# Second norm by pairs of token blocks, and three units of the up projection begun by products without sums

## The chip, the cores and the metric

The kernel runs on one core of a Trainium2 chip. Its engines are TensorE (PE, matmuls; the loading of its weights is shown as PEld), VectorE (DVE), ScalarE (ACT), GpSimd (POOL) and SyncE (SP), on whose queue all of the kernel's DMAs are issued. The metric is the device time of one execution in microseconds (us). A profile of one execution gives the start and length of each instruction.

## What is computed

One layer of a hybrid backbone on 1024 tokens of width 1024. Attention and retention with their gates make `merged`; after that, cut to what matters here:

```
x   = x + g1 * (merged @ w_out)                   # w_out 1024 x 1024
hx2 = rmsnorm(x) * norm2_g * (1 + sc2) + sh2      # the second norm
u   = hx2 @ w_up                                  # 1024 x (2 x 2816)
u   = centred conv of width 3 over tokens + bias
a, val = split(u);  y = (silu(a) * val) @ w_down  # 2816 x 1024
out = rmsnorm(x + g2 * y) * final_g
```

All of it is float32. A product of two float32 matrices is made of three matmuls on halves: each operand is split into a high part (rounded to the type fp32r) and a low part (what is left), and high x high, high x low and low x high are summed in PSUM.

## The kernel before, in words

**The output projection** (`out_proj`, L1638) takes eight blocks `tb` of 128 tokens. Each has two halves `dh` of 512 columns, each a chain of 8 x 3 matmuls of 128x512 into a bank `om` (two buffers in the pool `po`). DVE multiplies the bank by the gate into `xn` (L1650; two buffers of 128x1024), adds the residual into `x1` (L1651), SP stores `x1`, ACT squares it with a sum (L1654), DVE and POOL make the reciprocal root (L1655, L1656), and DVE writes the normed row into `xn` (L1657).

**The second norm** (`norm_out`, L1660) of block `tb-1` is written behind the whole of block `tb`. PE transposes the eight 128x128 squares of `xn` into two banks `tp` (L1671); for each, ACT writes the high part of scale times square plus shift (L1677), DVE writes the same as float32 into `v` (L1679) and from it the low part (L1680). The tokens are two halves: for half 0 (`h2[0]`, tile `h2a`) `v` is stored to `d_h`; for half 1 (`h2[1]`, tiles `h2h`, `h2l`) the `v` of the block four earlier is loaded into `vo`, and four differences (L1686 to L1689) of 128x512 make one block of T1, T2, T3 and T4, which SP stores to `d_t` (L1691).

**The up projection** runs over 22 units, in the order of `seq`; a unit is one block of 128 columns of the gate half (branch 0) and of the value half (branch 1) of `u`. The operand has four quarters, B11, B21 (half 0, the two halves of the contraction) and B12, B22 (half 1); the weights of a unit have four quarters a11, a12, a21, a22. A *plain* unit multiplies both branches by both halves: 4 chains of 8 x 3 matmuls, 96 of them, each into PSUM tiles of two banks (`u_tile`, L1709). The other units need seven products of 4 x 3 matmuls instead of eight (`Seven.step`, L1401, `Up`, L1789), 84 in all: POOL makes four sums s1 to s4 of the weights (L1383 to L1386), and the products are

- step 0: a11 B11 into bank X, copied by ACT to `p1` (L1408)
- step 1: s2 T2 into Y; DVE writes `u2` = Y + p1 (L1411)
- step 2: s1 T1 into Z
- step 3: s3 T3 onto Y; `u3` = Y + p1 (L1417); Z + u3 is the output of branch 1, half 1 (L1398)
- step 4: a12 B21 onto X, which is the output of branch 0, half 0 (copied by ACT, L1819)
- step 5: a22 T4 onto Y; Y + p1 is branch 1, half 0
- step 6: s4 B22 onto Z; Z + u2 is branch 0, half 1; then the convolution of the unit (`conv`, L1754: two ACT and two times two DVE passes, a silu, a product)

Steps of neighbouring units are interleaved: the sort key of step k of unit i is 7 i + 2 k (`interleaved`, L1434). Before each product ACT and DVE split its weights into a tile `wc` (L86, L87; six buffers). T1 to T4 are loaded from `d_t` and split once for all units (`comb`, L1780; tile `T`). Their raws, the weights and the sums of weights all take tiles of one pool, `ur` and `s` in the profile, with twelve slots that are given out in the order of the program (`ur_load`, L1733). `p1`, `u2`, `u3` and `h2h`, `h2l` are tiles of a pool of 17 (`gtile`, L1563, tag g).

The first two units are plain (`PLAIN = 2`). Half 0 of the first is written ahead of the norm of the last block (`early`), its half 1 and the whole second unit behind it; T2 and T1 are loaded in the first unit, T3 and T4 in the second.

**What sets the order.** The instructions are written down in the order of the program; a planner with a model of the times gives each engine its fixed order, and puts in the waits. On one engine an instruction that waits holds up all that stand behind it. An instruction wrapped in `late` stays at its place.

Of the kernel before, what the change touches and what calls it, by code (L numbers as in the profile page):

```python
# [40 lines left out]
def tile_hybrid_layer(ctx, tc: tile.TileContext, io, dbg=None):  # L41
# [18 lines left out]
    d_h = dram.tile([NTB // 2, P, KB, P], F32, name="d_h")  # L60
    d_t = dram.tile([4, NTB // 2, P, KB // 2, P], F32, name="d_t")
# [1314 lines left out]
    class Seven:  # L1376
# [24 lines left out]
        def step(self, n):  # L1401
# [7 lines left out]
            elif n == 1:  # L1409
                self.prod(self.Y, self.s2, "T2", True, False)  # L1410
# [219 lines left out]
    h2 = [[h2p.tile([P, 2, 512], F32R, tag="h2", bufs=KB, name="h2a") for _ in range(KB)], None]  # L1630
# [7 lines left out]
    def out_proj(tb):  # L1638
# [4 lines left out]
        for dh in range(2):  # L1643
            cs = slice(dh * 512, dh * 512 + 512)
            m = po.tile([P, 512], F32, tag="o", bufs=2, name="om")
            for kb in range(KB):
                wc = wo[kb, dh]
                h_, l_ = mg[kb, half]
                mm3(m, h_[:, ts], l_[:, ts], wc[:, 0], wc[:, 1], kb == 0, kb == KB - 1)
            vec.tensor_tensor(xr[:, cs], m, gate1[:, cs], ALU.mult)  # L1650
            vec.tensor_tensor(x1[:, cs], xr[:, cs], x1[:, cs], ALU.add)  # L1651
# [6 lines left out]
        return xr  # L1658

    def norm_out(tb, xr):  # L1660
        half, ts = tb // 4, slice((tb % 4) * P, (tb % 4 + 1) * P)
        if tb == 4:
            h2[1] = [(gtile(0, F32R, "h2h"), gtile(0, F32R, "h2l")) for _ in range(KB)]
        vr = op.tile([P, KB, P], F32, tag="v", bufs=2, name="v")
        if half:
            vo = op.tile([P, KB, P], F32, tag="vo", bufs=1, name="vo")
            sync.dma_start(vo, d_h[tb - 4])
        for kg in range(2):
            tp = po.tile([P, 4, P], F32, tag="t", bufs=2, name="tp2")
            for k in range(4):  # L1670
                pe.transpose(tp[:, k], xr[:, (kg * 4 + k) * P : (kg * 4 + k + 1) * P], ident)  # L1671
            for k in range(4):
                kb = kg * 4 + k
                t = h2[half][kb]
                h_, l_ = (t[:, 0, ts], t[:, 1, ts]) if half == 0 else (t[0][:, ts], t[1][:, ts])
                a, sh = a2[:, kb : kb + 1], col[:, 24 + kb : 25 + kb]
                act.activation(h_, tp[:, k], AF.Identity, bias=sh, scale=a)  # L1677
                v = vr[:, kb]
                vec.tensor_scalar(v, tp[:, k], a, sh, ALU.mult, ALU.add)  # L1679
                vec.tensor_tensor(l_, v, h_.bitcast(F32), ALU.subtract)  # L1680
        if half == 0:
            sync.dma_start(d_h[tb], vr)
            return

        (b11, b21), (b12, b22) = [(t[:, : KB // 2], t[:, KB // 2 :]) for t in (vo, vr)]
        vec.tensor_tensor(b11, b12, b11, ALU.subtract)  # L1686
        vec.tensor_tensor(b12, b22, b12, ALU.subtract)
        vec.tensor_tensor(b22, b22, b11, ALU.subtract)
        vec.tensor_tensor(b21, b21, b22, ALU.subtract)  # L1689
        for c, t in enumerate((b11, b22, b12, b21)):  # L1690
            sync.dma_start(d_t[c, tb - 4], t)  # L1691

    xr = None
    for tb in range(NTB):
        nx = out_proj(tb)
        if tb:
            norm_out(tb - 1, xr)
        xr = nx


    def up(u, wu, half):
        h = h2[half]
        hi, lo = ([t[:, i] for t in h] if half == 0 else [t[i] for t in h] for i in range(2))
        mm_a(u[:, half * 512 : half * 512 + 512], wu, lambda k: hi[k], lambda k: lo[k])

    def up_load(j, br):
        return [wload(io["w_up"][j, br, i]) for i in range(2)]

    def u_tile(n):  # L1709
        return pu[n // 2 % 2].tile([P, T], F32, tag="u", bufs=2, name="u")  # L1710

    early = []
    for br in range(2):
        early.append((u_tile(br), up_load(0, br)))
        up(*early[br], 0)
    norm_out(NTB - 1, xr)
# [63 lines left out]
    def comb(c):  # L1780
        t = [tpl.tile([P, 4, KH, P], F32R, name=f"T{c}{i}") for i in range(2)]
        for b in range(4):
            raw = ur_load(d_t[c, b])
            split(t[0][:, b], t[1][:, b], raw.rearrange("p (k t) -> p k t", k=KH))
# [4 lines left out]
    class Up(Seven):  # L1789


        def __init__(self, n, j):
            self.n, self.j = n, j
# [7 lines left out]

        def banks(self):
            t = u_tile(2 * self.n)
            self.X, self.Y = t[:, 0:512], t[:, 512:1024]
            self.Z = u_tile(2 * self.n + 1)[:, 0:512]
            self.u = [tap.tile([P, T], F32, tag="uu", bufs=4, name="uu") for _ in range(2)]

        def moving(self, c):
            if c[0] == "T":
                h_, l_ = combs[c]  # L1810
                return [(h_[:, :, k], l_[:, :, k]) for k in range(KH)]
            k0, half = HALVES[c]
            return [(t[:, 0], t[:, 1]) if half == 0 else t for t in h2[half][k0 : k0 + KH]]

        def dst(self, b, half):
            return self.u[b][:, half * 512 : half * 512 + 512]
# [4 lines left out]
        def done(self, b, half):  # L1821
            if (b, half) == (0, 1):
                conv(self.j, *self.u)
# [11 lines left out]
    seq = [j + NH * i for j in range(NH) for i in range(2)]  # L1835
# [251 lines left out]
```

## Time and profile before

| what | us |
|---|---|
| three runs | 1766.35, 1765.24, 1760.98 |
| median | 1765.24 |
| profiled execution, first to last instruction (span; the only time kept of it) | 1759.2 |
| output projection, first matmul to last (`om`) | 1007.8 to 1100.8 |
| plain units, first matmul to last | 1101.6 to 1147.8 |
| first product by sevens | 1147.6 |

The profile lists, for each engine, groups of instructions as `line engine operation tile<-operands`, with count, busy time and mean length; waits as `who <- for whom`; and timelines, where a row is start, length, engine, line, operation, with the idle time before it and what ended it in brackets. The length of a matmul contains its way through the array, so that one starts before the other has ended; from start to start is what a matmul costs in a row of them. Times are counted from the first instruction.

### The profile page before, as it was taken

The numbers are of one execution on the slowest core, as the hardware profiler recorded it, in microseconds if no ns is written. First come the engines' busy times: TensorE is split into PE (matmuls) and PEld (weight loads), VectorE is DVE, ScalarE is ACT, GpSimd is POOL, SyncE is SP. The second block draws the span as 40 slices with busy tenths as digits, with TensorE's granted clock in tenths as the row PEclk, the third lists the DMA queues.
The fourth block names the chain that finished last, engine by engine and source line by source line (L and its number), as shares of the span: only waits on it lengthen the run. The fifth ranks groups of instructions, "written<-read, shape, count | busy, mean of one in ns | idle before, by whom it ended". The sixth has DMA issues, their size and how long they took to land.

```text
span 1759.2 us, 24801 instructions
## 1 busy us (share of the span) xinstructions
PE 1726.0 (98%) x8405; PEld 1429.3 (81%) x8405; DVE 1284.2 (73%) x2454; ACT 849.2 (48%) x1826; POOL 539.3 (31%) x455
## 2 busy tenths in 40 slices
PE   8999999999999999999999999989999999999997
PEld 4688988888888888778888888778888888788886
DVE  4778887756776766777665557868899889875755
ACT  5666666653443434443444324534444444554444
POOL 1000000003334343555413300165555655211444
PEclk9999999999999999999999999999999999999999
DMA  9143334342231212677557733733322332586754
GB/s 348 61 130 125 95 117 147 117 133 87 73 108 43 72 42 68 203 238 239 200 199 268 246 143 132 254 108 102 108 90 92 118 120 90 170 296 192 239 162 162
DMA packets 139408, 261.10 MB, mean 148 GB/s; under 512 B 15856, under 2 KB 28304, under 8 KB 139280
## 3 DMA queue, kind: packets, MB, share of 16 engines
q1 hardware_dynamic: 139280, 259.51, 44.3%
q8 instruction: 66, 1.08, 0.3%
q14 instruction: 62, 0.51, 0.1%
HBM read 187.34 MB, written 69.48 MB: 146 GB/s over the span
## 4 chain that ended last, share of the span: by engine, by line
PE 43%; issue 6%; DVE 4%; POOL 3%; DMA 1%; ACT 1%; SPq 0%; POOLq 0%; ACTq 0%; DVEq 0%
PE u L1374 30%; PE y L1374 4%; PE pr L112 2%; PE pr L111 2%; PE pr L110 2%; PE om L122 1%; PE om L121 1%; PE om L123 1%; POOL x L1902 1%; DVE wc L87 0%; DVE b L1350 0%; DVE v L1679 0%; POOL pd L1939 0%; DVE hxT L87 0%; POOL x L1947 0%
## 5 line engine op out<-in xcount | busy, mean ns | idle before, releaser
L1374 PE MATMUL u<-T,wc 128*128 128x512 f32 x960 | 227.1, 392 | 5.1 <-ACT pu L1408 5.1
L1374 PEld LDWEIGHTS u<-T,wc 128*128 128x128 f32 x960 | 180.6, 189 | 45.7 <-ACT pu L1408 7.9
L1374 PE MATMUL y<-wc,ahl 128*128 128x512 f32 x924 | 210.6, 389 | 2.7 <-DVE wc L87 1.8
L1374 PEld LDWEIGHTS y<-wc,ahl 128*128 128x128 f32 x924 | 173.3, 188 | 39.7 <-DVE wc L87 2.5
L87 DVE TENSOR_TENSOR wc<-ur,wc 128x512 fp32r<-128x512 f32 x137 | 122.7, 897 | 65.8 <-ACT wc L86 65.8
L86 ACT CAST wc<-ur 128x512 fp32r<-128x512 f32 x137 | 85.0, 621 | 129.7 <-PE y L1374 72.3
L111 PE MATMUL mm<-low,wc 128*128 128x512 f32 (+1 forms) x328 | 124.0, 378 | 0.0
L1374 PE MATMUL u<-h2a,wc 128*128 128x512 f32 x480 | 112.3, 389 | 0.7 <-DVE pu L1417 0.7
L110 PE MATMUL mm<-hx,wc 128*128 128x512 f32 x264 | 107.4, 407 | 0.2 <-ACT wc L589 0.2
L1374 PEld LDWEIGHTS u<-h2a,wc 128*128 128x128 f32 x480 | 90.0, 188 | 19.8 <-DVE pu L1417 1.2
L112 PE MATMUL mm<-hx,wc 128*128 128x512 f32 x264 | 105.2, 399 | 0.0
L86 ACT CAST wc<-s 128x512 fp32r<-128x512 f32 x80 | 49.7, 623 | 93.2 <-PE u L1374 88.3
L123 PE MATMUL mm<-wc,low 128*128 128x512 f32 (+1 forms) x240 | 91.2, 380 | 0.0
L1374 PE MATMUL u<-hxT,wc 128*128 128x512 f32 x384 | 89.6, 389 | 0.0
L1508 POOL TENSOR_TENSOR col<-col,bcol 128x32 f32<-128x32 f32 x1 | 0.3, 253 | 280.7 <-DVE aw L538 280.7
L87 DVE TENSOR_TENSOR wc<-s,wc 128x512 fp32r<-128x512 f32 x80 | 83.5, 1046 | 3.8 <-ACT wc L86 3.4
L1374 PEld LDWEIGHTS u<-hxT,wc 128*128 128x128 f32 x384 | 72.1, 188 | 14.9
L87 DVE TENSOR_TENSOR wc<-raw,wc 128x512 fp32r<-128x512 f32 x92 | 68.0, 746 | 17.7 <-ACT wc L86 17.7
L121 PE MATMUL mm<-wc,hx 128*128 128x512 f32 x192 | 75.2, 392 | 0.6 <-ACT r L1105 0.6
L122 PE MATMUL mm<-wc,hx 128*128 128x512 f32 x192 | 75.2, 392 | 0.0
L1383 POOL TENSOR_TENSOR s<-ur 128x512 f32<-128x512 f32 x20 | 35.7, 1783 | 126.3 <-DVE wc L87 68.7
L86 ACT CAST wc<-raw 128x512 fp32r<-128x512 f32 x92 | 56.8, 621 | 33.0 <-PE pr L112 6.0
(393 smaller groups left out, 4671.3 us busy)
## 6 DMA issues: line engine op xcount, KB each, us to landing
ur<-in_w_up SPq DMA_DIRECT2D x80, 256.0 KB, 2.9
ur<-d_a SPq DMA_DIRECT2D x77, 256.0 KB, 3.1
aw<-in_w_ada SPq DMA_DIRECT2D x32, 512.0 KB, 3.3
pj<-in_w_down SPq DMA_DIRECT2D x44, 256.0 KB, 5.2
d_w<-pj SPq DMA_DIRECT2D x44, 256.0 KB, 2.0
d_a<-sa SPq DMA_DIRECT2D x44, 256.0 KB, 2.0
ur<-d_w SPq DMA_DIRECT2D x44, 256.0 KB, 3.8
d_a<-at SPq DMA_DIRECT2D x33, 256.0 KB, 2.7
```

Of the source, the lines that this page charges most:

```text
L86: act.copy(hi, src)
L87: (lo_eng or vec).tensor_tensor(lo, src, hi.bitcast(F32), ALU.subtract)
L110: pe.matmul(out, wh, xh, start=k == 0, stop=False)
L111: pe.matmul(out, wh, xl, start=False, stop=False)
L112: pe.matmul(out, wl, xh, start=False, stop=k == n - 1)
L121: pe.matmul(out, ah, bh, start=first, stop=False)
L122: pe.matmul(out, ah, bl, start=False, stop=False)
L123: pe.matmul(out, al, bh, start=False, stop=last)
L1374: pe.matmul(out, a, b, start=first and n == 0, stop=last and n == 2, skip_group_check=True)
L1383: pool.tensor_tensor(self.s1, self.a21, self.a22, ALU.add)
L1508: pool.tensor_tensor(col[:, 16:48], col[:, 16:48], bcol[:, 16:48], ALU.add)
L1902: pool.tensor_tensor(z, z, fg[:, gs(dh)], ALU.mult)
```

## The change

The norm works on pairs of blocks: `norm_out(g)` takes the two `xn` of the blocks 2g and 2g+1 in four pieces. A piece transposes four squares (two of each block) into one bank and then handles two stretches of 128x256; the differences are 128x1024 and are stored right behind one another's making, each with rows of 256 elements. `out_proj` is written in four pieces too, and one piece of the norm of the pair before stands behind each. `xn` keeps its two buffers. The high and low parts of half 1 are made for the lower half of the contraction alone (B22), since no unit multiplies by B12 any more.

All 22 units use seven products. Of the first three (`HEADS`), the two products that need no sum (steps 0 and 4: a11 B11, a12 B21) are written ahead, behind the last block of the output projection, with the norm of the last pair between them: `head(n)` multiplies a11 B11 into a bank, copies it to `p1`, and multiplies a12 B21 onto the same bank. Then unit 0's weights are loaded and summed, T2, T1, T3, T4 are loaded, and the interleaved steps begin, without steps 0 and 4 of those three units. X gets three banks of its own and Y, Z five, one bank each; the tiles `uu` become five.

```diff
-    d_h = dram.tile([NTB // 2, P, KB, P], F32, name="d_h")
-    d_t = dram.tile([4, NTB // 2, P, KB // 2, P], F32, name="d_t")
+    d_h = dram.tile([NTB // 4, P, KB, 2 * P], F32, name="d_h")
+    d_t = dram.tile([4, KB // 2, P, 512], F32, name="d_t")
...
             elif n == 1:
+                if not self.loaded:
+                    self.load()
+                if not hasattr(self, "Y"):
+                    self.yz()
+                    self.u2, self.u3 = self.tmp(), self.tmp()
...
                 mm3(m, h_[:, ts], l_[:, ts], wc[:, 0], wc[:, 1], kb == 0, kb == KB - 1)
+                if kb == 3 or (kb == 7 and dh == 0):
+                    yield
...
-        return xr
+        xrs.append(xr)
+        yield
+
+    W2 = 2 * P
+
+    def norm_out(g, xrs):
+        half, c0 = g // 2, g % 2 * W2
+        if g == 2:
+            for kb in range(KH, KB):
+                h2[1][kb] = (gtile(0, F32R, "h2h"), gtile(0, F32R, "h2l"))
+        vr = op.tile([P, KB, W2], F32, tag="v", bufs=1, name="v")
         if half:
+            vo = op.tile([P, KB, W2], F32, tag="vo", bufs=1, name="vo")
+            sync.dma_start(vo, d_h[g - 2])
+        for k2 in range(KH):
+            tp = po.tile([P, 2, W2], F32, tag="t", bufs=3, name="tp2")
+            kbs = (k2, k2 + KH)
+            for i, kb in enumerate(kbs):
+                for n, xr in enumerate(xrs):
+                    pe.transpose(tp[:, i, n * P : (n + 1) * P], xr[:, kb * P : (kb + 1) * P], ident)
+            for i, kb in enumerate(kbs):
                 a, sh = a2[:, kb : kb + 1], col[:, 24 + kb : 25 + kb]
                 v = vr[:, kb]
+                hl = h2[half].get(kb) if half else (h2[0][kb][:, 0], h2[0][kb][:, 1])
+                if hl:
+                    act.activation(hl[0][:, c0 : c0 + W2], tp[:, i], AF.Identity, bias=sh, scale=a)
+                vec.tensor_scalar(v, tp[:, i], a, sh, ALU.mult, ALU.add)
+                if hl:
+                    vec.tensor_tensor(hl[1][:, c0 : c0 + W2], v, hl[0][:, c0 : c0 + W2].bitcast(F32), ALU.subtract)
+            yield
...
+        for c, o, x, y in ((0, b11, b12, b11), (2, b12, b22, b12), (1, b22, b22, b11), (3, b21, b21, b22)):
+            vec.tensor_tensor(o, x, y, ALU.subtract)
+            sync.dma_start(d_t[c, :, :, c0 : c0 + W2].rearrange("k p t -> p k t"), o)
+
+    HEADS = 3
+    seq = [j + NH * i for j in range(NH) for i in range(2)]
+    heads = {}
+
+    def u_tile():
+        return pu[0].tile([P, 512], F32, tag="u", bufs=3, name="u")
+
+    def head(n):
+        bank, p1 = u_tile(), gtile(0, F32, "pu")
+        for i in range(2):
+            w = wload(io["w_up"][seq[n], 0, i])
+            for k in range(KH):
+                h = h2[0][k + KH * i]
+                open3(bank, w[:, 0, k * P : (k + 1) * P], w[:, 1, k * P : (k + 1) * P], h[:, 0], h[:, 1], k == 0 and i == 0, k == KH - 1 and i == 1)
+            if i == 0:
+                act.copy(p1, bank)
+        heads[n] = bank, p1
+
+    xrs, norm = [], iter(())
     for tb in range(NTB):
-        nx = out_proj(tb)
-        if tb:
-            norm_out(tb - 1, xr)
-        xr = nx
...
-    early = []
-    for br in range(2):
-        early.append((u_tile(br), up_load(0, br)))
-        up(*early[br], 0)
-    norm_out(NTB - 1, xr)
+        for _ in out_proj(tb):
+            next(norm, None)
+        if tb % 2:
+            norm = norm_out(tb // 2, xrs[tb - 1 :])
+    for n in range(HEADS):
+        head(n)
+        for _ in norm if n else range(1):
+            next(norm, None)
...
     def comb(c):
+        t = [tpl.tile([P, KH, 512], F32R, name=f"T{c}{i}") for i in range(2)]
+        for k in range(KH):
+            split(t[0][:, k], t[1][:, k], ur_load(d_t[c, k]))
         return t
...
+        def yz(self):
+            self.Y, self.Z = (pu[1].tile([P, 512], F32, tag="u", bufs=5, name="u") for _ in range(2))
+
         def banks(self):
+            self.X = u_tile()
+            self.yz()
+
+        def begin(self, bank, p1):
+            self.X, self.p1 = bank, p1
+            self.c11()
...
-    PLAIN = 2
-
-    for n, j in enumerate(seq[:PLAIN]):
-        us2 = []
-        for br in range(2):
-            u, wu = (u_tile(2 * n + br), up_load(j, br)) if n else early[br]
-            for half in range(2) if n else (1,):
-                up(u, wu, half)
-            us2.append(u)
-        for c in ((1, 0), (2, 3))[n]:
-            combs[f"T{c + 1}"] = comb(c)
-        conv(j, *us2)
     units = [Up(n, j) for n, j in enumerate(seq)]
-    for i, n in interleaved(PLAIN, NF):
-        units[i].step(n)
+    units[0].load()
+    for c in (1, 0, 2, 3):
+        combs[f"T{c + 1}"] = comb(c)
+    for n in range(HEADS):
+        units[n].begin(*heads[n])
+    for i, n in interleaved(0, NF):
+        if i >= HEADS or n not in (0, 4):
+            units[i].step(n)
```

More of the change, by code (lines that the diff above doesn't have):

```diff
@@ L1629, in tile_hybrid_layer @@
     h2p = sb("h2", "left")
-    h2 = [[h2p.tile([P, 2, 512], F32R, tag="h2", bufs=KB, name="h2a") for _ in range(KB)], None]
+    h2 = [[h2p.tile([P, 2, 512], F32R, tag="h2", bufs=KB, name="h2a") for _ in range(KB)], {}]
     op = sb("outp", "right")
@@ L1810, in moving @@
                 h_, l_ = combs[c]
-                return [(h_[:, :, k], l_[:, :, k]) for k in range(KH)]
+                return [(h_[:, k], l_[:, k]) for k in range(KH)]
             k0, half = HALVES[c]
-            return [(t[:, 0], t[:, 1]) if half == 0 else t for t in h2[half][k0 : k0 + KH]]
+            return [(h2[0][k][:, 0], h2[0][k][:, 1]) if half == 0 else h2[1][k] for k in range(k0, k0 + KH)]
         def dst(self, b, half):
-            return self.u[b][:, half * 512 : half * 512 + 512]
+            return self.out(b)[:, half * 512 : half * 512 + 512]
         def c11(self):
```

52 lines of the change are left out of this document (7 added, 45 removed).

## The prediction, made before the changed kernel had run

> **What bounds the kernel now.** I read the page first, then the list of PE's waits, the windows, and the timelines of PE, DVE, ACT, POOL and SP from 1000 to 1185 us, where the changed code runs.
>
> ```profile
> span 1759.2 us, 24801 instructions
> PE 1726.0 (98%) x8405; PEld 1429.3 (81%) x8405; DVE 1284.2 (73%) x2454; ACT 849.2 (48%) x1826; POOL 539.3 (31%) x455
> ```
> ```profile
> PE u L1374 <- ACT pu L1408: 5.1, 1, 5.1
> ```
> ```profile
> 1080.00:1100.00 20.00, 20.00 (x93) 16.55 (x92) 17.27 (x46) 8.94 (x20) 1.09 (x2) 1.00 0.35 133
> 1150.00:1160.00 10.00, 4.85 (x15) 3.59 (x14) 6.54 (x8) 4.18 (x6) 5.48 (x4) 0.83 0.59 184
> 1300.00:1400.00 100.00, 100.00 (x440) 82.05 (x439) 89.94 (x90) 44.88 (x63) 53.84 (x30) 1.00 0.28 92
> ```
>
> The columns of the windows are length, then busy time of PE, its weight loads, DVE, ACT and POOL, then granted clock, DMA share and GB/s. PE is full nearly everywhere, so a matmul saved is time saved, provided PE stays fed. The up projection has one hole, at 1150 to 1160, and with it a clock of 0.83. DVE is the next engine: 90% in the steady loop of products.
>
> ```profile
> 1100.77 1.03 PE L1671 MATMUL tp<-ident,xn 128*128 128x128 f32 x8
> 1113.68 0.73 PE L110 MATMUL u<-h2h,wc 128*128 128x512 f32 x2
> 1114.77 0.50 PE L111 MATMUL u<-h2l,wc 128*128 128x512 f32 x1 [0.35 <-DVE h2l L1680]
> 1125.87 0.39 PE L110 MATMUL u<-h2a,wc 128*128 128x512 f32 x1
> ...
> 1147.63 2.88 PE L1374 MATMUL u<-h2a,wc 128*128 128x512 f32 x12
> 1150.35 1.07 PE L1374 MATMUL u<-T,wc 128*128 128x512 f32 x4
> 1156.57 9.09 PE L1374 MATMUL u<-T,wc 128*128 128x512 f32 x32 [5.15 <-ACT pu L1408]
> 1165.49 5.60 PE L1374 MATMUL u<-h2a,wc 128*128 128x512 f32 x24
> ```
>
> From 1125.87 to 1147.63 lie 96 matmuls of one plain unit: 0.2267 us each; the 0.39 of a row overlaps the next one. From 1100.77 to 1125.87 PE issues 96 matmuls (21.8) and 16 transposes in 25.1 us. After the hole 32 matmuls take 8.92 us where 7.25 would do: 1.7 us for the low clock. Line L110 twice running, ahead of L111, tells that the planner doesn't keep the written order on PE: what its model holds ready goes first, by place in the program among the ready ones.
>
> ```profile
> 1148.02 10.13 SPq L1735 DMA_DIRECT2D ur<-in_w_up x8
> ```
> ```profile
> 1152.85 0.62 ACT L86 CAST wc<-ur 128x512 fp32r<-128x512 f32 x1 [4.21 <-DMA ur<-in_w_up]
> ...
> 1155.93 0.58 ACT L1408 COPY pu<-u 128x512 f32<-128x512 f32 x1
> ```
> ```profile
> 1139.52 5.42 POOL L1383 TENSOR_TENSOR s<-ur 128x512 f32<-128x512 f32 x1 [33.12 <-DMA ur<-in_w_up]
> ...
> 1151.61 1.26 POOL L1383 TENSOR_TENSOR s<-ur 128x512 f32<-128x512 f32 x1 [1.92 <-DMA ur<-in_w_up]
> ```
>
> The hole is made in queues: POOL's first sum takes 5.42 us instead of 1.26, the twelve slots of `ur` come free late, the loads go out at 1148, ACT stands 4.21 us at the cast of such a load, and the copy of p1, for which PE waits, is queued behind that cast.
>
> **The change part by part.** *Matmuls.* Two plain units are 192 products of 128x512, two units by seven products 168. 24 fewer, times 0.2267: **-5.4**. The three heads (72) only move.
>
> *The hole.* Plain units and the start of unit 2 after them are gone, so this hole goes with its clock: **-5.2 and -1.7**. The waits of the plain half 1 for the last block's norm also go: 25.1 less 21.8, less two groups of eight transposes at 0.94 (next fence), is **-1.5**.
>
> ```profile
> 1018.55 0.39 PE L123 MATMUL om<-wx,ml 128*128 128x512 f32 x1
> 1018.78 0.39 PE L121 MATMUL om<-wo,mh 128*128 128x512 f32 x1
> ```
> ```profile
> 1029.72 1.04 PE L1671 MATMUL tp<-ident,xn 128*128 128x128 f32 x8
> ...
> 1041.60 1.03 PE L1671 MATMUL tp<-ident,xn 128*128 128x128 f32 x8
> ```
> ```profile
> 1018.98 0.69 DVE L1650 TENSOR_TENSOR xn<-om,gate 128x512 f32<-128x512 f32 x1 [4.08 <-PE om L123]
> ...
> 1022.43 0.75 DVE L1657 TENSOR_SCALAR xn<-x,ss 128x1024 f32<-128x1024 f32 x1 [0.66 <-POOL ss L1656]
> ```
>
> *Transposes.* A token block without transposes takes 10.94 us (1018.78 to 1029.72), with eight 11.88: 0.94 per group, of which about 0.8 are the eight and 0.14 the switch. There are as many transposes, but 16 groups of four for 8 of eight: 8 x 0.14 = **+1.1**.
>
> *A new wait in the output projection.* `xn` still has two slots, and both rows of a pair are read until the fourth group of transposes, which is written behind all 48 matmuls of the next block. That block's first eviction (L1650) writes a third `xn`, so it waits for the fourth group; both `om` banks are then full, and the block after cannot start.
>
> ```profile
> 1077.10 1.03 PE L1671 MATMUL tp<-ident,xn 128*128 128x128 f32 x8
> ...
> 1077.80 0.46 ACT L1677 ACTIVATE h2h<-tp,col,a 128x128 fp32r<-128x128 f32 x1 [5.54 <-PE tp L1671]
> ```
>
> A group is done 0.7 us after its start, of which 0.4 is issue; a running DVE instruction (0.2), the eviction (0.69) and the handover make 1.2 us of PE idle, at blocks 2, 4 and 6. At 4 and 6 the first head's matmuls, whose weights and rows are there, can fill it; at 2 nothing can: **+1.3**. The output projection ends 3.6 us later, ten matmuls of heads done in it.
>
> *The way to the first sum operand.* This is the main price. Before, a whole plain unit (21.8 us) covered the trip of T1 to T4 through memory; now only the heads do. The last `xn` is ready 4.2 us after the last matmul of its block (1018.94 to 1023.18). The first group follows; groups two to four are written behind the second head, and slip into the gap while its p1 is copied (0.58 and handovers), or wait for its second half: the fourth starts 7.3 to 10.1 us after the output projection's end.
>
> ```profile
> L1763 DVE TENSOR_TENSOR at<-ta,at 128x1024 f32<-128x1024 f32 x22 | 26.7, 1214 | 0.0
> L1679 DVE TENSOR_SCALAR v<-tp,a,col 128x128 f32<-128x128 f32 x64 | 24.6, 406 | 1.5 <-ACT h2h L1677 0.8 <-ACT h2a L1677 0.6
> L87 DVE TENSOR_TENSOR T<-ur,T 128x512 fp32r<-128x512 f32 x16 | 10.2, 684 | 2.3 <-ACT T L86 2.3
> L1680 DVE TENSOR_TENSOR h2l<-v,h2h 128x128 fp32r<-128x128 f32 x32 | 8.5, 286 | 0.2
> ```
> ```profile
> 1122.99 2.08 DMA d_t<-v
> ```
> ```profile
> d_x<-x SPq DMA_DIRECT2D x8, 512.0 KB, 2.8
> ```
> ```profile
> 1125.13 0.80 SPq L1735 DMA_DIRECT2D ur<-d_t x2
> ...
> 1126.92 6.10 SPq L1735 DMA_DIRECT2D ur<-d_t x11
> ```
> ```profile
> 1127.75 1.29 ACT L86 CAST T<-ur 128x512 fp32r<-128x512 f32 x2 [0.17 <-DMA ur<-d_t]
> ```
>
> From 286 ns at 128 columns to 684 at 512 is 1.04 ns a column, so 256 columns cost DVE 0.54 (L1679) and 0.42 (L1680); a 128x1024 difference costs 1.21. Behind the fourth group: 0.7, two v, one low part and three differences (T2's is the third) 5.1, the store 2.8 (256 KB took 2.08; the 512 KB row stands nearest), the load 2.6 (1125.13 to 1127.75), cast and split 1.3, handovers 0.2: 12.7 us. T2 reaches PE 20.0 to 22.8 after the output projection; I take 21.5. PE has 62 matmuls (14.05) and four groups (2.2) for it, 16.2: idle **+5.3**, and as long a gap cost 1.7 of clock before: **+1.7**. Bounds: 1 us if all groups slip in early and the store takes 2.08, 9 us if they come last.
>
> *Behind it.* Sixteen T loads at 0.55 to 0.7 us each (eleven went out in 6.10) keep pace with 0.68 us of PE per block of three matmuls; DVE has four splits, an add and a weight split in the 2.72 us of one product: **+1.0** in all (0 to 3). Unit 1's four loads stand behind all sixteen in the order of the slots. Counted from the first T load: sixteen loads at 0.7 and three of unit 1, 13.3, landing 2.6, two sums on POOL at 1.26, cast and split 1.3 make 19.7 for its s2; unit 0's five products end at 2.6 + 1.3 + 13.6 + 1.0 = 18.5. That is 1.2, and with queueing I take **+2.5** (0, to 8 by the 5.42 row).
>
> *At nothing.* DVE loses 64 x (406 + 286) ns for 32 x 0.54 + 24 x 0.42 us, 17 us less, in a stage where PE is full and DVE has room (17.27 of 20); it would cost only if PE waited there. The six added weight loads go under the output projection (DMA share 0.35); uncovered 0.7 each. More `uu` and bank slots serve a loop whose PE is at 100 of 100.
>
> *Sum:* -5.4 -5.2 -1.7 -1.5 +1.1 +1.3 +5.3 +1.7 +1.0 +2.5 = **-0.9 us**. On the profiled span of 1759.2 that is 1758.3; the median run stands 6.0 above that span, which I keep: **1764.3**.
>
> **The rivals.** *The trip of T2 hides (faster).* The planner puts all four groups right behind the last `xn`, and unit 1 is in time: idle falls from 5.3 to 1.3, clock loss 1.7 and the 3.5 behind it go: -0.9 - 9.2 = -10.1, 1755. For it: the model orders by readiness, and the only waits it misjudged around the norm are small (0.35). Against it: two heads are written before the last three groups.
>
> *A blocked queue again (slower).* POOL's sums for unit 1 fall among the T4 splits and unit 0's convolution on DVE, as the first sum did at 1139.52. At 5.42 for one and a late load, s2 comes 5 us later, ACT stands before its cast, and the copies behind it hold PE: +5.2, and 1.7 for the clock: +6.0 in all, 1771. It decides where s2 of unit 1 ends later than unit 0's fifth product. For it: the same code did this before with a full plain unit as cover. Against it: unit 0's sums are made early, beside the heads. The Trainium skill (SBUF — State Buffer, "Who interferes with whom") says that a DVE instruction with two SBUF inputs and a GpSimd instruction that reads SBUF exclude each other, the second blocking until the first is done. By that rule each of those sums waits for splits, and this rival would be likelier than I set it; the 5.42 row agrees, the 1.26 row shows a sum that met none.
>
> *The order isn't moved as I think.* If the groups of transposes stay at their written places, PE meets the first 2.7 us after a block's end with `xn` 4.2 after it: 1.5 at three pairs, +4.5, 1769.
>
> **How the numbers follow.** This kernel's runs tell a change from none at about 0.3%, 5.3 us. The forecast (no change) has 0.38, with its own range 1759 to 1770, of which 0.04 reaches to faster and 0.03 to slower; the hidden trip 0.32 (0.02 of it within); the blocked queue 0.22 (0.01 within); the unmoved order 0.08, half within. Faster 0.34, same 0.38, slower 0.28. The range of 8 in 10 takes in both sides: 1753.5 (gain 11.7, near the best of the bounds: no idle for T2, none behind) to 1774 (T2 last or POOL at 5.42 throughout).
>
> **What would show it.** PE after the change with 24 matmuls fewer in `u`; a gap of some 1.2 us ahead of the fourth block of the output projection, released by L1650; one gap of about 5 us ahead of the first T product, released by the split of T; a smaller one ahead of unit 1's first product; none at `pu`. Wrong if PE waits at the transposes for `xn`, if the first T product follows the heads without a gap, or if a gap of over 5 us stands later, released by ACT or POOL.

## The result, and the profile after

The changed kernel takes 1777.57 us (median of four runs, 1776.16 to 1779.2) against 1765.8 of the kernel before: ratio 1.0075, interval 1.006 to 1.0089. It is slower by 0.75%; forecast were 1764.3 and a range to 1774. The profiled execution is the one of 1776.16. First the page, the longest waits of PE in the changed part, and windows with the columns of before.

```profile
span 1774.4 us, 24687 instructions
PE 1727.1 (97%) x8381; PEld 1428.2 (80%) x8381; DVE 1296.0 (73%) x2390; ACT 840.9 (47%) x1796; POOL 555.0 (31%) x463
```
```profile
PE u L1374 <- ACT T L86: 8.7, 1, 8.7
PE u L1374 <- ACT wc L86: 4.8, 1, 4.8
...
PE tp L1684 <- DVE xn L1664: 2.0, 4, 0.7
PE u L1374 <- DVE pu L1422: 2.0, 1, 2.0
```
```profile
1120.00:1130.00 10.00, 4.88 (x21) 3.38 (x19) 8.71 (x11) 3.99 (x8) 2.88 (x2) 1.00 0.41 137
1130.00:1140.00 10.00, 5.25 (x11) 3.39 (x12) 3.40 (x5) 4.40 (x8) 0.00 (x0) 0.55 0.95 311
1140.00:1150.00 10.00, 6.86 (x27) 4.91 (x25) 8.34 (x12) 5.91 (x10) 2.12 (x2) 0.94 0.80 296
1150.00:1160.00 10.00, 7.67 (x21) 5.66 (x22) 10.00 (x8) 3.84 (x7) 9.84 (x7) 0.66 0.40 114
```

The 24 matmuls are gone (8405 to 8381), and so is the old hole behind `pu` L1408. In its place stand three: ahead of the first T product, ahead of unit 1's first product (a cast of its weights), and a wait for `u3` (L1422), which has to read bank Y before the next product goes onto it. PE's timeline shows each with its releaser:

```profile
1107.21 1.07 PE L1374 MATMUL u<-h2a,wc 128*128 128x512 f32 x4
...
1123.07 3.01 PE L1374 MATMUL u<-h2a,wc 128*128 128x512 f32 x12 [1.20 <-ACT pu L1719]
1134.76 7.25 PE L1374 MATMUL u<-T,wc 128*128 128x512 f32 x16 [8.67 <-ACT T L86]
1142.27 4.86 PE L1374 MATMUL u<-T,wc 128*128 128x512 f32 x20 [0.27 <-DVE T L87]
1151.95 1.22 PE L1374 MATMUL u<-T,wc 128*128 128x512 f32 x2 [4.82 <-ACT wc L86]
1153.55 10.19 PE L1374 MATMUL u<-T,wc 128*128 128x512 f32 x34 [0.38 <-DVE wc L87]
...
1173.86 7.30 PE L1374 MATMUL u<-T,wc 128*128 128x512 f32 x24 [1.97 <-DVE pu L1422]
```

The first T product comes 27.5 us after the output projection's end (1107.2); 21.5 were forecast. The sixteen matmuls from there on take 7.25 us, at a clock near a half. They and the twenty at 1142.27 are unit 0's three products with T2, T1 and T3. SP's, POOL's and ACT's rows show why unit 1 is late: its loads leave at 1142.85, behind all sixteen T loads, its first sum starts at 1147.80, and the cast of its s2, released by the second sum, at 1151.28.

```profile
1126.39 2.10 SPq L1702 DMA_DIRECT2D d_t<-v  x2
1129.39 0.36 SPq L1702 DMA_DIRECT2D d_t<-vo  x1
1131.24 0.82 SPq L1750 DMA_DIRECT2D ur<-d_t  x2
...
1133.11 9.46 SPq L1750 DMA_DIRECT2D ur<-d_t  x14
1142.85 34.21 SPq L1750 DMA_DIRECT2D ur<-in_w_up  x16
```
```profile
1147.80 1.77 POOL L1383 TENSOR_TENSOR s<-ur 128x512 f32<-128x512 f32 x1 [24.93 <-DMA ur<-in_w_up]
```
```profile
1151.28 0.62 ACT L86 CAST wc<-s 128x512 fp32r<-128x512 f32 x1 [4.73 <-POOL s L1384]
```

**The balance of the two profiled executions.** From the first `om` matmul to the end of the span, before takes 751.4 us (1007.8 to 1759.2), after 765.7 (1008.7 to 1774.4): +14.3. Between 1020 and 1200 PE stands still 20.0 us by the windows, before 5.8: +14.2. The low clock behind the three gaps costs 3.6 (16 matmuls in 7.24 us where 3.63 would do), 3.1 (36 in 11.24, for 8.16) and 1.7 (24 in 7.14, for 5.44), before 1.7: +6.7. The matmuls saved are -5.4, and -1.9 lies in the steady loop (below). That makes +13.6; the +0.7 that is left stands near the 1.1 forecast for the transposes.

### The profile page after: what moved, and what is told of

Same layout as the page of the kernel before. It is cut to its first block, busy times and chain, and to the rows that moved or that the text cites. A ratio compares the mean times of both kernels' runs of the same rounds, so it can differ in the third digit from the quotient of the medians.

```text
span 1774.4 us, 24687 instructions
## 1 busy us (share of the span) xinstructions
PE 1727.1 (97%) x8381; PEld 1428.2 (80%) x8381; DVE 1296.0 (73%) x2390; ACT 840.9 (47%) x1796; POOL 555.0 (31%) x463
## 4 chain that ended last, share of the span: by engine, by line
PE 43%; issue 7%; DVE 4%; POOL 3%; ACT 1%; DMA 1%; SPq 0%; POOLq 0%; DVEq 0%; ACTq 0%
PE u L1374 31%; PE y L1374 4%; PE pr L112 2%; PE pr L111 2%; PE pr L110 2%; PE om L123 1%; PE om L122 1%; PE om L121 1%; DVE wc L87 1%; POOL x L1919 0%; DVE b L1350 0%; DMA ur<-in_w_up 0%; POOL pd L1956 0%; PE tp L1684 0%; POOL pd L1955 0%
## 5 line engine op out<-in xcount | busy, mean ns | idle before, releaser
L1374 PE MATMUL u<-T,wc 128*128 128x512 f32 x1056 | 255.1, 398 | 16.1 <-ACT T L86 8.7
L1374 PEld LDWEIGHTS u<-T,wc 128*128 128x128 f32 x1056 | 202.5, 192 | 62.0 <-ACT T L86 9.5
L86 ACT CAST wc<-ur 128x512 fp32r<-128x512 f32 x137 | 84.9, 622 | 110.2 <-PE y L1374 70.7
L1374 PE MATMUL u<-h2a,wc 128*128 128x512 f32 x528 | 125.1, 391 | 1.2 <-ACT pu L1719 1.2
L1374 PEld LDWEIGHTS u<-h2a,wc 128*128 128x128 f32 x528 | 98.5, 188 | 22.4 <-ACT pu L1719 2.2
L86 ACT CAST wc<-s 128x512 fp32r<-128x512 f32 x88 | 54.3, 621 | 99.2 <-PE u L1374 86.9
L87 DVE TENSOR_TENSOR wc<-s,wc 128x512 fp32r<-128x512 f32 x88 | 96.0, 1093 | 1.2 <-ACT wc L86 0.9
L86 ACT CAST wc<-raw 128x512 fp32r<-128x512 f32 x90 | 55.7, 621 | 32.2 <-PE mm L112 5.0
```

The lines of the kernel that those rows point to most:

```text
L86: act.copy(hi, src)
L87: (lo_eng or vec).tensor_tensor(lo, src, hi.bitcast(F32), ALU.subtract)
L1374: pe.matmul(out, a, b, start=first and n == 0, stop=last and n == 2, skip_group_check=True)
```

## The experiments

All times are medians; ratio and 95% interval are to the kernel before, run beside each. That kernel's own median moved between 1763.95 and 1765.8 from one set of runs to another, and in the profiles here the output projection starts anywhere from 1007.7 to 1011.8 us, ahead of all changed code. Where two runs differ by 3 us or less, their intervals overlap, and the difference alone proves nothing. In t_elsewhere, space_else, no_T and T_near the operand is not the layer's, and no_tlow leaves out the low parts of T: these runs give times, not results.

| run | us | ratio | interval |
|---|---|---|---|
| after | 1777.57 | 1.0075 | 1.0060 to 1.0089 |
| pairs_only | 1773.18 | 1.0047 | 1.0032 to 1.0061 |
| heads_only | 1771.86 | 1.0041 | 1.0027 to 1.0055 |
| t_elsewhere | 1772.98 | 1.0049 | 1.0034 to 1.0063 |
| space | 1778.85 | 1.0087 | 1.0074 to 1.0100 |
| space_else | 1774.30 | 1.0059 | 1.0047 to 1.0071 |
| fill | 1778.26 | 1.0076 | 1.0063 to 1.0089 |
| u1_first | 1776.24 | 1.0076 | 1.0064 to 1.0088 |
| heads4 | 1776.04 | 1.0065 | 1.0052 to 1.0077 |
| no_tlow | 1777.18 | 1.0074 | 1.0061 to 1.0087 |
| by_pair | 1774.52 | 1.0059 | 1.0045 to 1.0073 |
| all3 | 1774.16 | 1.0055 | 1.0042 to 1.0067 |
| xn3 | 1780.14 | 1.0090 | 1.0076 to 1.0104 |
| no_T | 1759.66 | 0.9975 | 0.9965 to 0.9984 |
| T_near | 1766.91 | 1.0014 | 1.0005 to 1.0023 |
| one_plain | 1770.99 | 1.0041 | 1.0029 to 1.0053 |
| before_u2first | 1760.14 | 0.9979 | 0.9970 to 0.9989 |
| pairs_u2first | 1769.85 | 1.0033 | 1.0022 to 1.0045 |
| before_plain1 | 1772.77 | 1.0043 | 1.0030 to 1.0057 |

**The theory to begin with:** the heads cover less than the plain units did, T2's way through memory shows, and its gap and low clock are the loss. Rivals: the pair norm and its waits in the output projection; DVE's load; the order of the loads.

### The two halves of the change

pairs_only puts the two plain units back (with half 1's high and low parts for all eight squares); heads_only puts the block norm back.

```diff
-    for n in range(HEADS): head(n) ...
+    two plain units, half 0 of the first ahead of the norm, as before   # pairs_only
-    norm_out(g) in pieces
+    norm_out(tb - 1) by blocks; the last one behind head(0)             # heads_only
```

> The pair norm, the output projection in four pieces and the stores of T by pairs of blocks are kept, but two plain units stand ahead of the products by sevens, as in the kernel before. If the loss comes from the lost cover (only three heads stand where 21.8 us of plain products stood behind the norm), the time comes back to the kernel before, 1765.8, within 4 us: 1762 to 1770. If the pair norm itself, with its waits for xn and its longer chain, is what costs, the loss stays: 1774 or more.

> The other half of the change alone: the norm by single blocks as before, three heads in place of the plain units, the last block's norm behind the first head. By the theory of lost cover the loss stays, somewhat less than with pairs since three quarters of each T are stored earlier and the last block's stores are 256 KB: 1770 to 1778, with a gap of 4 to 8 us ahead of the first T product. By the theory that the pair norm costs it, 1764 or less.

Both parts cost: +7.9 us and +6.5 us, against +11.8 for the whole. heads_only is as the theory of lost cover had it (7.1 us of gap ahead of the first T product). pairs_only lies between its two cases and speaks against lost plain work as the only cause: all plain units are there, and the hole of before comes back larger, made as before by a late weight (3.5 us at `wc` L86, 3.2 at the convolution's `ta`).

### The trip of T2

```diff
-            split(t[0][:, k], t[1][:, k], ur_load(d_t[c, k]))
+            split(t[0][:, k], t[1][:, k], ur_load(io["w_up"][c, k % 2, k // 2]))   # t_elsewhere
```

> The changed kernel, but T1 to T4 are loaded from blocks of the weights, which lie in memory from the start, instead of from what the norm has stored; sizes, splits and products are the same, the stores are still made, and the output is not the layer's. If the trip of T2 through memory makes the 8.67 us gap and its low clock (3.6 us), and the T loads hold up unit 1's loads (4.8 us and 3 of clock), both go with it: 1758 to 1766. If the gap comes from DVE and ACT being busy with the norm's last pieces, or from the pair norm ahead of it, the time stays within 3 us of 1777.6.

Only 4.6 us come back, between the two cases and at the edge of what the intervals can tell, and 6.1 us of gap stay ahead of T2. In ACT's row the cast of T2 is released by the store of T4:

```profile
1133.33 5.83 ACT L86 CAST T<-ur 128x512 fp32r<-128x512 f32 x11 [10.10 <-DMA d_t<-vo]
```

T2's tile is laid out on the memory of `v` and `vo`, which the norm's last stores still read: a second wait behind the first, 0.8 us earlier (0.3, counted in each run from the start of the output projection). The next two runs take this away, alone and with the trip.

```diff
+    place = {c: [tpl.tile([P, KH, 512], F32R, ...) for i in range(2)] for c in (3, 2, 0, 1)}
-        t = [tpl.tile([P, KH, 512], F32R, name=f"T{c}{i}") for i in range(2)]
+        t = place[c]                                   # space; with the line above: space_else
```

> The changed kernel with the eight T tiles laid out in another order, T4's first: in the changed kernel T2's tile lies on the memory of the norm's v and vo, so that its first cast also has to wait until T4's store has left vo (in t_elsewhere the cast is released by that store at 1133.3, in the changed kernel by the load at 1134.1). Theory: the two ways to T2 end within a microsecond of each other, and with the trip through memory still there nothing changes: 1775.5 to 1779. If the memory under T2 was what held it up, 4 us or more come back: below 1773.

> Both at once: the T tiles in the other order, and T1 to T4 loaded from blocks of the weights, so that nothing of the norm's end holds up T2 (output is not the layer's). If trip and memory together make the gap ahead of T2, that gap and its clock go (t_elsewhere kept 6.1 us of gap): 1761 to 1768. If what is left in t_elsewhere is DVE's and ACT's queue, the time stays at 1771 to 1775.

space changes nothing that can be told, as expected. space_else lies in its second case: the first T product starts at 1130.09, nearly without a gap, yet the time is no better than t_elsewhere. The wait has moved to `u2`, which stands on DVE behind fifteen of the sixteen splits:

```profile
1130.09 0.40 PE L1374 MATMUL u<-T,wc 128*128 128x512 f32 x1
1132.70 4.18 PE L1374 MATMUL u<-T,wc 128*128 128x512 f32 x17 [2.21 <-DVE T L87]
...
1145.91 4.38 PE L1374 MATMUL u<-T,wc 128*128 128x512 f32 x11 [6.53 <-DVE pu L1416]
```

```diff
+    junk = pu[1].tile([P, 512], F32, ...)
+    for n in range(32): pe.matmul(junk, ...)           # fill, behind units[0].load()
```

> The changed kernel with 32 matmuls more (7.25 us at full clock) written behind the heads, whose results nobody uses, into a bank of their own. They lie in the 8.67 us in which PE waits for T2. If the low clock after the gap is a cost of its own, caused by PE's standing still, some 3 us come back: 1773 to 1775.5. If the clock is not tied to the gap, the time stays at 1777 to 1778. If PE did not really stand still, 7 us are added: 1784.

7.25 us of matmuls more cost 0.7 us, so the gap was idle; but the time doesn't fall either, although the sixteen matmuls behind the gap now take 5.84 us where they took 7.24. The gap ahead of T2 shrinks to 2.7, those ahead of unit 1 and of `u3` grow to 5.4 and 2.8. A PE that arrives sooner waits longer: something behind T2 sets the end. The first theory, that gap plus clock are the loss, has fallen.

### Single cures behind it

```diff
     for c in (1, 0, 2, 3):
+        if c == 3: units[1].load()                     # u1_first
-    HEADS = 3
+    HEADS = 4                                          # heads4; X 4 banks, Y and Z 4, tp 2
-            split(t[0][:, k], t[1][:, k], ur_load(d_t[c, k]))
+            act.copy(t[:, k], ur_load(d_t[c, k]))      # no_tlow
-    d_t = dram.tile([4, KB // 2, P, 512], ...)
+    d_t = dram.tile([4, 2, P, KB // 2, 2 * P], ...)    # by_pair; loads [c, pair, :, k:k+2]; tiles as in space
```

> The changed kernel with unit 1's four weight loads and four sums written ahead of the last four T loads instead of behind them. If unit 1's sums are late because its loads stand behind sixteen T loads, the 4.8 us gap ahead of unit 1's first product shrinks to 2 us or less, and with its clock 3 to 6 us come back: 1772 to 1775. If POOL's sums are slow because DVE is full of splits, not because the loads are late, less than 2 us: 1776 to 1778.

> The changed kernel with four heads instead of three (24 more useful products written ahead, 5.45 us; X has four banks, Y and Z four, the transposes two). fill showed that junk in the gap ahead of T2 gains nothing. If what counts is the moment when loads, splits and sums have caught up, and how much useful product work PE has done by then, the whole 5.45 come back: 1770.5 to 1773.5. If those later waits move along with what PE does, or the tighter banks cost it, less than 2 us: 1775.5 to 1779.

> The changed kernel without the sixteen DVE subtractions that make the low parts of T1 to T4 (the high part is used in their place; the matmuls are as many, the output is not float32-exact). If DVE, 90 to 100% busy from 1150 on, carries a backlog that holds PE after T2, its 9.8 us of splits are worth 4 to 10 us: 1767 to 1773. If DMA and the order of the loads set the end, less than 2: 1775.5 to 1778.

> The changed kernel with T stored and loaded by pairs of blocks, as the kernel before did by blocks: each load carries 256 tokens of two squares in place of 512 tokens of one, so that eight of the sixteen loads, casts and splits need only the pair before the last, and stand ahead of unit 0's loads; T's tiles lie as in space. If the sixteen loads behind the last store, and the splits behind them, are what makes the transition long, unit 1's loads and DVE's splits come 4 to 5 us sooner: 1771 to 1774. If not, 1776 to 1780, as with the tiles' order alone.

u1_first and heads4 lie in their second cases: 1.3 and 1.5 us come back by the medians, less than the intervals can tell. In u1_first the gap ahead of unit 1 does shrink, to 2.3, but that ahead of `u3` grows from 2.0 to 2.7. heads4 is fill with useful work: the gap ahead of T2 falls from 8.67 to 2.10, and PE waits 5.42 for unit 1 and three times for `u3` instead:

```profile
PE u L1374 <- DVE pu L1422: 5.9, 3, 2.8
PE u L1374 <- ACT wc L86: 5.4, 1, 5.4
```

no_tlow clears DVE's load: without sixteen splits nothing changes. by_pair, which lets half of T go ahead of the norm's end, gives 3.1 us by the medians, just short of its first case; the two intervals overlap.

```diff
all3: by_pair and u1_first and heads4
-        xr = op.tile([P, D], F32, tag="xn", bufs=2, ...)
+        xr = op.tile([P, D], F32, tag="xn", bufs=3, ...)   # xn3; x1 from 3 to 2
```

> The changed kernel with three cures at once: T by pairs of blocks (by_pair), unit 1's loads ahead of T4's (u1_first), four heads (heads4). Singly they gave back 3.1, 1.3 and 1.5 us. If several chains of nearly equal length end the transition, together they give more than their sum: 1764 to 1770. If each gives its own share and no more, 1771 to 1773; if one untouched chain sets the end, 1774 or more.

> The changed kernel with three slots of xn (and two of x1 in place of three): the third block's first eviction waits no more for the fourth group of transposes. The prediction put this wait at 1.3 us; the trace shows 0.67 at L1657 and 2.0 at the transposes in four places. If waits in the output projection count one for one: 1774 to 1776. If what PE saves there it waits later for T2: 1777 to 1778.

all3 is no better than by_pair, its third case: cures of several places don't add up. That one untouched chain sets the end is what that case supposed; the run doesn't show which. xn3 shortens the output projection by 2.8 us (95.9 for 98.7 from its first matmul to the end of its last) and gains nothing: the third head waits 3.7 us for its p1 instead of 1.2, and T2 comes 126.9 us after the projection's start, in the changed kernel 126.1. The time lies above both of its cases. Of the 2.6 us that it is longer than the change, nothing can be laid to `xn`: in the two profiles the projection itself starts 2.6 us later (1011.3 for 1008.7), and `x1` has lost a slot besides.

### All of T away, and the way through memory alone

```diff
-                h_, l_ = combs[c]
+                return [(h2[0][k][:, 0], h2[0][k][:, 1]) for k in range(KH)]            # no_T; comb not called
-            split(t[0][:, k], t[1][:, k], ur_load(d_t[c, k]))
+            split(t[0][:, k], t[1][:, k], h2[1][KH + k][0].bitcast(F32))                # T_near
```

> The changed kernel with the rows of half 0 as operand in place of T1 to T4: as many matmuls, but no T loads, casts and splits, and nothing of the norm's last pair that the products wait for (the output is not the layer's; the differences are still made and stored). If the transition's 25 us of waiting all hang on T (trip, memory, loads, splits), PE runs on from the heads: 1750 to 1758. If the weights and sums of units 1 and 2 are a chain of their own of nearly the same length, 1760 to 1770.

> The changed kernel with T1 to T4 cast and split from rows that the norm's last piece leaves in SBUF (the high parts of half 1) instead of from loads of d_t; as many casts, splits and matmuls, the differences and stores are still made, nothing waits for them (the output is not the layer's); T's tiles lie as in space. no_T gave 1759.7. If the way through memory is T's price, the time comes near that: 1759 to 1765. If ACT's and DVE's sixteen casts and splits are, it stays at 1770 to 1776.

no_T gives back 17.9 us, between its two cases: the loss hangs on T. T_near splits that sum, and falls between its cases: 10.7 us are the way through memory, 7.2 the rest. Its timeline tells which part of that way:

```profile
1128.13 0.50 PE L1374 MATMUL u<-T,wc 128*128 128x512 f32 x1 [1.90 <-ACT T L86]
1136.17 19.14 PE L1374 MATMUL u<-T,wc 128*128 128x512 f32 x71 [7.54 <-DVE T L87]
```
```profile
1122.96 1.47 POOL L1383 TENSOR_TENSOR s<-ur 128x512 f32<-128x512 f32 x1
...
1128.03 1.72 POOL L1386 TENSOR_TENSOR s<-ur,s 128x512 f32<-128x512 f32 x1
```

PE still stands 9.4 us around the first T product (after: 8.67 and 0.27), here for splits behind the differences on DVE. But from 1136 on it runs without a gap: unit 1's sums are made at 1123 to 1130, 25 us sooner than in the changed kernel, because no T loads stand ahead of its weights in the twelve slots. So the 10.7 us are not the gap at T2. t_elsewhere, which takes away the wait for the stores and keeps the sixteen loads, gave 4.6 of them; the other 6 or so come with the loads themselves, which unit 1 and the units behind it have to let pass. This division is an estimate, since T_near also changes the order on ACT and DVE. u1_first moved unit 1's loads past four of the sixteen; past all sixteen was not tried.

### How much cover the products by sevens want

```diff
+    plain(...) for unit 0, head(1) alone, sevens from unit 1     # one_plain, from the changed kernel
-    PLAIN = 2
+    PLAIN = 1                                                    # before_plain1, with units[1].load() ahead of T
         for c in ((1, 0), (2, 3))[n]:
+        if n: units[2].load()  (ahead of that loop)              # before_u2first; pairs_u2first on pairs_only
```

> The pair norm with one plain unit (12 matmuls more, 2.7 us) and one head: behind the norm of the last pair stand 48 plain products and the head's 24 where the change has 48 of heads, so 27 us of work cover the way to T2 in place of 16. By the theory of lost cover the gap ahead of T2 (8.7) and its clock (3.6) go for the most part, and unit 1's stays: 1768 to 1773. If cover isn't what is missing, the 2.7 us are added: 1778 to 1782.

> The kernel before with one thing moved: unit 2's four weight loads and sums are written ahead of the T3 and T4 loads instead of behind them. If the 5.15 us hole of the kernel before is the late load of its first product's weights, it goes with its clock: 1757.5 to 1761. If POOL's first sum (5.42 us, while DVE splits) is what holds it, it stays: 1763 to 1767.

> pairs_only (pair norm, two plain units) with unit 2's loads and sums ahead of those of T3 and T4, as in before_u2first, which took 3.8 us off the kernel before. If the pair norm costs 7.9 us because it pushes these loads further back into the products by sevens, most of it goes: 1760 to 1765. If it costs them in the output projection (waits for xn, 3 us) and in the longer chain to T2, the cure is worth what it was worth before: 1768 to 1771.

> The kernel before with one plain unit in place of two (12 matmuls fewer, 2.7 us), no heads, the block norm, and the next unit's loads and sums ahead of T's, as in before_u2first (1760.1). If cover is what the products by sevens need behind the norm, 21.8 us less of it cost more than the 2.7 us saved: 1762 to 1772. If the block norm's way of storing three quarters of T early makes the second plain unit needless: 1756.5 to 1758.5.

one_plain has 12 matmuls more than the change and is 6.6 us faster, as lost cover would have it. before_u2first **beats both kernels**: 3.8 us faster than before, 17.4 faster than the change. No wait over 1.4 us is left in its up projection:

```profile
PE u L1374 <- DVE pu L1411: 1.4, 1, 1.4
...
PE u L1374 <- ACT pu L1408: 1.0, 1, 1.0
```

So the hole of before was the order of loads: it needed one load moved and no heads. On the pair norm the same move is worth 3.3 us by the medians, as its second case said, with intervals that overlap; 9.7 us then still part the pair norm from the block norm. before_plain1 lies just above its first case: against before_u2first it saves 2.7 us of matmuls and loses 12.6, so the 21.8 us of the second plain unit are worth 15.3. Not all of that is cover for T: 4.4 us are a wait of the remaining plain unit for the last block's own rows (L1680), where before had waits of 0.6 there.

## Why the prediction was wrong, step by step

- **Matmuls, -5.4:** right.
- **The old hole and its clock, -6.9:** it did go, but before_u2first, which removes it from the kernel before, gains 3.8. A little of what PE gains there it waits for again (1.4 and 1.0 at `pu`).
- **The waits for the last block's norm, -1.5:** gone with the plain units; 1.20 stands at the third head instead (below).
- **The wait for `xn`, +1.3, and its transposes, +1.1:** a wait of 0.67 at L1657, and 2.0 in four places at the transposes, which the prediction named as a sign against itself. The projection is 5.6 us longer (98.7 for 93.1), with eight head matmuls in it; 3.6 and ten were forecast. xn3 shows that these us don't count by themselves.
- **The way to T2, +5.3 and +1.7:** mechanism right, sizes wrong: the gap is 8.67, with 1.20 ahead of the third head's second half, and the clock 3.6. The fourth group of transposes stood 11.5 us after the projection's end instead of 7.3 to 10.1, and what follows took 16.0 us instead of 12.7. The store, the load and the splitting took what was forecast (6.7 us for 6.9); T2's difference was made late, at 1128.1, some 9.5 us after the group's start where 5.8 were counted. One reason is a queue that the prediction didn't look at: ACT stands before the casts of unit 0's sums, with two of the norm's activations behind them. DVE, too, has splits of unit 0's weights between the norm's last instructions (1.12, 0.68 and 0.68 us).

```profile
1119.97 1.14 ACT L86 CAST wc<-s 128x512 fp32r<-128x512 f32 x2 [3.58 <-POOL s L1384]
1121.01 1.01 ACT L1690 ACTIVATE h2h<-tp,col,a 128x256 fp32r<-128x256 f32 x2
```

```profile
1126.89 1.21 DVE L1701 TENSOR_TENSOR v<-v,vo 128x1024 f32<-128x1024 f32 x1
```

  Gaps and clock measure 13.5 us here (8.67, 1.20 and 3.6), and 7.0 were forecast. From T_near to no_T are 7.2 us, but that this lies near 7.0 is luck: T_near's gap waits for splits and not for the trip, and no_T leaves out the casts and splits as well.
- **What follows, +1.0 and +2.5: this is the step that failed.** The prediction wrote "Unit 1's four loads stand behind all sixteen in the order of the slots", counted 1.2 and took 2.5. The time of unit 1's s2 it had nearly right: its product starts 20.7 us after the first T load (1151.95 and 1131.24), and 19.7 were counted. What it set against this was wrong: "unit 0's five products", of 13.6 us. By the sort key 7 i + 2 k unit 1's step 1 has key 9, and unit 0's steps 5 and 6 have 10 and 12, so that only three products (keys 2, 4 and 6) stand ahead of it. PE's rows show just these, 16 and 20 matmuls, and then the wait. With three products the prediction's own terms give 2.6 + 1.3 + 8.2 + 1.0 = 13.1, and a wait of 6.6 in place of 1.2. In the profile 12.2 us stand where +1.0 and +2.5 were forecast: 4.82 ahead of unit 1, 1.97 at `u3`, 0.27 and 0.38, and 4.8 of low clock behind the two larger. With the T loads and all that they hold back taken away (T_near) 10.7 come back. Besides, the count ended with unit 1; but unit 2's sums follow in the same slots and on the same POOL, and `u3`, L1398 and the convolution in the same queue of DVE, so that a delay can be met again at later steps, as the wait at `u3` shows.
- **"At nothing", the banks of the steady loop:** wrong the other way. The starts of step 6 of three units running, before and after:

```profile
1198.36 0.39 PE L1374 MATMUL u<-h2l,wc 128*128 128x512 f32 x1
...
1217.40 0.39 PE L1374 MATMUL u<-h2l,wc 128*128 128x512 f32 x1
...
1236.69 0.39 PE L1374 MATMUL u<-h2l,wc 128*128 128x512 f32 x1
```
```profile
1197.54 0.39 PE L1374 MATMUL u<-h2l,wc 128*128 128x512 f32 x1
...
1216.58 0.39 PE L1374 MATMUL u<-h2l,wc 128*128 128x512 f32 x1
...
1235.62 0.39 PE L1374 MATMUL u<-h2l,wc 128*128 128x512 f32 x1
```

  19.04 and 19.29 in turn before, 19.04 each after: 84 x 0.2267 is 19.04. Over the loop that is a gain of about 1.9 us (0.096 a unit, some twenty units). heads_only has 19.04 as well, pairs_only 19.13 in the mean, so it comes with the heads' half of the change; whether with its banks or with the fifth `uu` was not told apart. "PE at 100 of 100" hid it: a matmul's record is 0.39 us long and covers a stop of 0.16.
- **Span and median:** the 6.0 us between profiled span and median were not an offset. In every run here that shows both, the time lies 1.8 above the span (1776.16 and 1774.4 in the changed kernel), so the profile of before, at 1759.2, is that of its fastest run, 1760.98. Part of the 15.2 us between the two profiles is this.
- **The rivals:** the blocked queue (1771, chance 0.22) named the place, unit 1's sums on POOL; the sums took 1.6 to 1.8 us and not 5.42, the loads were late. Its condition counts the same five products. The exclusion that the Trainium skill states (SBUF — State Buffer, "Who interferes with whom") shows in T_near, where one sum, begun inside DVE's unbroken row of sixteen splits, ends 1.15 us behind the row (1146.30 and 1145.15); unit 0's first sum, ahead of the splits, took 1.28:

```profile
1138.70 7.60 POOL L1383 TENSOR_TENSOR s<-ur 128x512 f32<-128x512 f32 x1 [8.95 <-DMA ur<-in_w_up]
```
```profile
1135.44 9.71 DVE L87 TENSOR_TENSOR T<-h2h,T 128x512 fp32r<-128x512 f32 x16
```

  The hidden trip (0.32) was the wrong way round: the groups came later, not sooner. The unmoved order (0.08) is seen in part: 2.0 us at the transposes, where 4.5 were its price.

What stays open: why the pair norm with full cover still costs 9.7 us against the block norm. 5.5 us are the output projection, which takes longer from its first matmul to its last (98.6 in pairs_only, 93.1 before), partly for plain products done inside it; how the rest divides between the longer chain of the last pair and T loads that all wait for it was not told apart. That the delay is met again at unit 1 and at `u3` is read from the traces of the change, fill, u1_first and heads4; no run follows one unit alone, and none puts unit 1's loads ahead of all sixteen T loads.

## What to carry to other kernels

When work that a slow chain hides behind is taken away, don't price the first gap alone: list everything that was loaded, summed and split under that cover for the *next* units too, in the order in which they share slots and queues, for any of these may be late in its turn; and read from the program's own order which products really stand in front of the one that has to wait. If single cures (fill the gap, shorten the trip, relieve an engine) each give little, take the whole suspect away once (no_T) and then give half of it back (T_near). And before replacing work by less work, look whether the hole in it is an order of loads: one load moved gave 3.8 us here.

## What the runs showed of the hardware

The clock falls and recovers some time after PE stops and starts. Windows of 2 us of the changed kernel, around the first and the last gap:

```profile
1130.00:1132.00 2.00, 0.00 (x0) 0.00 (x0) 0.00 (x0) 0.00 (x0) 0.00 (x0) 0.73 1.00 339
...
1138.00:1140.00 2.00, 2.00 (x5) 1.33 (x5) 1.66 (x3) 1.84 (x4) 0.00 (x0) 0.50 0.99 366
1140.00:1142.00 2.00, 2.00 (x7) 1.23 (x5) 1.07 (x2) 1.74 (x4) 0.00 (x0) 0.71 1.04 397
...
1174.00:1176.00 2.00, 2.00 (x8) 1.66 (x9) 2.00 (x3) 1.02 (x1) 0.00 (x0) 0.82 0.00 0
1176.00:1178.00 2.00, 2.00 (x6) 1.52 (x6) 1.34 (x3) 1.83 (x3) 0.00 (x0) 0.50 0.21 26
```

PE stops at 1126.1, and the granted clock falls to a half within 1130 to 1132; PE starts again at 1134.76, and the clock is full at about 1141, 6 us later. Around the gap of 1.97 us that ends at 1173.86 it falls too, when PE has already started again. The Trainium skill (TensorE: Matmul & The Clock Gate, "Part 1: The HAM clock gate") gives about 4 us of steady work until the full clock, and a fall after an idle window of about 3.4 us; here it took 6, and a fall followed a gap of 1.97.
